# A fixed order for the seven products of a projection pair, a third buffer for weight splits, and three transfers moved

## The chip, the cores and the metric

The kernel runs on one core of a Trainium2 chip. The metric is the time of one execution on the device in microseconds (us). Engines are called as the profile calls them: PE (TensorE, matmuls; PEld is its weight load), DVE (VectorE), ACT (ScalarE), POOL (GpSimd) and SP (SyncE, which here only issues transfers). L353 is line 353 of the kernel before.

## What is computed

One inference step of a two-layer hybrid encoder. 512 prompt rows and 8 x 16 sample rows share the weights and are handled as T = 640 rows of width 1024. Cut to what matters here:

```python
for l in range(DEPTH):                      # DEPTH = 2
    (a_u, a_v, a_g, b_x, b_g, c_q, c_kv, c_kr, c_g, m_q, gate_logits) = split_cols(x @ w_in)
    oa = gelu(a_u) * mix(layer_norm(gelu(a_v))) * silu(a_g)      # gated mixing in chunks of 128
    ob = rglru(b_x) * silu(b_g)                                  # convolution of 4 + a recurrence
    oc = mla(c_q, c_kv, c_kr) * silu(c_g)                        # latent attention, past keys cached
    om = mem_attend(m_q, mem_k, mem_v)                           # memory attention, caches for samples
    g = sigmoid(gate_logits)                                     # four gates of 1024 columns
    merged = g[0]*(oa@w_br_a) + g[1]*(ob@w_br_b) + g[2]*(oc@w_br_c) + g[3]*(om@w_br_m)
    x = layer_norm(ALPHA * x + merged @ w_out)
```

## The kernel before

Every product is made three times in a reduced 32-bit format: a number is split into a high and a low part, and high x high, high x low and low x high are added. The split of a weight is done by `split` (L144): ACT casts the raw weight into `wh`, and DVE subtracts to get `wl` (L147). The buffers of `raw` are three, those of `wh`, `wl` and `ws` two each. Weights come on SP's queue, nearly all else (scratch in HBM written and read back) on POOL's queue, which works in its own order together with POOL's computations.

Most projections are taken two at a time by `fm_pair` (L353). It computes two chunks of 128 output rows for all 640 columns with seven products in place of eight, from sums of weights (DVE, L360) and sums of x (`xt`, computed once for each layer and kept in HBM as `xsum`). Each product is 12 matmuls of 128 x 320. In the order of the code they are, with the names used from here on:

- P1: x half 11 with `r0`, into `ba`, the first half of the accumulator tile `fp`; ACT then copies `ba` to `p1` (`tu`, L383).
- P2: x half 21 with `r0`, into `bb`, the second half of the same tile `fp`; DVE then adds z0 = p1 + bb (L377).
- P3: `xt[2]` with `ws`, added into `ba`; ACT copies it to `u` (`tu`, L392).
- P4: `xt[3]` with `ws`, into the separate bank `fp_c`; ACT copies it to z1 (L394).
- P5: `xt[1]` with `r1`, added into `ba`; DVE subtracts it from z1 (L377).
- P6: `xt[4]` with `r1`, added into `fp_c`; DVE forms the other half of z1 (L377).
- P7: x half 22 with the second half of `r0`, added into `ba`.

The accumulators `acc` (L80) are two tiles, shared by the pairs, the branch products `y`, the mixing `mix` and the single chunks `fm`. There are 40 pairs, 20 in a layer. Six stand in the front of the layer, in this order: two of u (`gelu_pair`, L419), two of gate C (`silu_pair(1, ...)`, L407), then the mixing, then two of gate B (`silu_pair(2, ...)`). Fourteen stand in the merge (`merge_pairs`, L1043): each computes two gate chunks and is followed by the branch products `y` of the same two chunks (48 matmuls of 128 x 320; 24 for the memory branch) and their multiply-adds on DVE. In PE's instruction order the products of a pair are woven into one another by a scheduler; the order section below shows it.

Between front and merge lie the latent attention, then the memory attention for the samples (four loads `mcache` of 1 MB from SP's queue, L809, in the three buffers of the pool `kv`), the recurrence (`lru_in`, `lru_gates`, `lru_rest` for four chunks), the memory attention for the prompt, and single chunks and products of the first merge branch. In the front, the u branch is written to scratch by `gelu_pair`, read back in four pieces `ub` (L566), multiplied with the mixed values and written back; pieces, copies `tu`, `mixb` and `th` share a pool of five buffers of 128 x 640 (`tmp`, L71). Gate B is read back as one tile `ob` of 4 x 640 (L804) for the whole recurrence, in the pool `o` in which the four reloaded `xt` (`x_sums_back`, L343, 1.25 MB each) also stand.

Of the kernel before, what the change touches and what calls it, by code (L numbers as in the profile page):

```python
# [22 lines left out]
NB = 8  # L23
# [16 lines left out]
def encoder_step(  # L40
# [65 lines left out]
    def whl(raw, n=1024):  # L106
        h, lo = wtile("wh", n, "wh"), wtile("wl", n, "wl")
        split(h, lo, raw)
        return h, lo
# [53 lines left out]
    def after(ins_, dep):  # L163
        tc.add_manual_dep(
            ins_.ins, dep.ins.name,
            mybir.DependencyInfo(mybir.DependencyClass.Sync, mybir.DependencyReason.DATA),
            reason="concurrent tiles of the array are issued together",
        )

# [9 lines left out]
    def spill(bi, k, src):  # L179
        nc.gpsimd.dma_start(out=oscr[bi][k], in_=src)  # L180
# [9 lines left out]
    for l in range(L):  # L190
# [66 lines left out]
        def w_c(c):  # L257
            if l > 0:
                r = wload(ins["w_c"][l, c], 832)
                x_sums(1)  # L260
                return r
            if c > 0:
                r = wload(ins["w_c"][l, c], 832)
                x_in(2 * c, 2)
                return r
            raw = wp.tile([128, 832], F32, tag="raw", name="raw", bufs=3)
            h = wp.tile([128, 832], F32R, tag="wh", name="wh")
            lo = wp.tile([128, 832], F32R, tag="wl", name="wl")
            for j in range(2):
                js = slice(416 * j, 416 * j + 416)  # L270
                nc.sync.dma_start(out=raw[:, js], in_=ins["w_c"][l, c][:, js])
                x_in(j, 1)
                split(h[:, js], lo[:, js], raw[:, js])
            return h, lo
# [68 lines left out]
        def x_sums_back():  # L343
            for i in range(4):
                t_ = otile([128, 2, 4, TH], F32R, f"xt{i}")
                nc.gpsimd.dma_start(out=t_.bitcast(F32), in_=xsum[i])
                xt[i + 1] = t_[:, 0], t_[:, 1]
# [5 lines left out]
        def fm_pair(c, take):  # L353

            r0, r1 = (wraw(ins["w_fm"][l, c + e]) for e in range(2))
            ws = wtile("ws", 1024, "ws")
# [8 lines left out]
            def product(o, hl, half, x, first, last):  # L365
# [3 lines left out]
                for n, (k, a, b) in enumerate(steps):  # L369
                    k0 = half * 512 + k * 128  # L370
                    PE.matmul(  # L371
                        out=o, lhsT=a[:, k0:k0 + 128], rhs=b[:, k, :],
                        start=(first and n == 0), stop=(n == len(steps) - 1), skip_group_check=True,
                    )

# [43 lines left out]
        def gelu_pair(c):  # L419
            gs = []  # L420
            z = fm_pair(FM_U + c, lambda e, cols, v_: gs.append((e, cols, v_)))
            for e, cols, v_ in gs:
                ACT.activation(out=z[e][:, cols], in_=v_, func=AF.Gelu_apprx_tanh)
            for e in range(2):
                nc.gpsimd.dma_start(out=gscr[0][c + e], in_=z[e])
# [75 lines left out]

        for c in (0, 2):
            gelu_pair(c)


        am = atile([128, 2560], F32, "am")
# [51 lines left out]
        for c in range(4):  # L558
# [6 lines left out]
            th, ub = tmp([128, T], "mixb"), tmp([128, T], "ub")  # L565
            nc.gpsimd.dma_start(out=ub, in_=gscr[0][c])  # L566
# [10 lines left out]
            DVE.tensor_tensor(out=ub, in0=ub, in1=th, op=ALU.mult)  # L577
            nc.gpsimd.dma_start(out=gscr[0][c], in_=ub)
# [218 lines left out]
        ob = gate_back(2, "ob")  # L797
# [9 lines left out]
        for bp in range(4):  # L807
            kv = kvtile([128, 2, 2, 2, 256], F32, "mcache")
# [75 lines left out]
        def lru_in(c):  # L884
            xp = lb[c % 2][:, 0, :]
# [45 lines left out]
        def lru_rest(c):  # L931
# [15 lines left out]
            DVE.tensor_tensor(out=ob[:, c, 0:NP_], in0=ob[:, c, 0:NP_], in1=xc[:, 0:NP_], op=ALU.mult)  # L947
            obs = ob[:, c, NP_:T].rearrange("p (b t) -> p b t", b=NB)
            DVE.tensor_tensor(out=obs, in0=obs, in1=samp(lb[c % 2][:, 1, :])[:, :, 0:TS], op=ALU.mult)
            spill(1, c, ob[:, c, :])  # L950
# [171 lines left out]
        lnp = [wtile("ws", 1024, f"lnp{i}") for i in range(2)]  # L1122
# [172 lines left out]
```

## Time and profile before

| what | value |
|---|---|
| three runs | 1450.77, 1454.91, 1456.23 us |
| median | 1454.91 us |
| the profiled execution itself | 1456.32 us, of which span 1454.6 us |
| busy share of the span | PE 96 %, DVE 68 %, ACT 45 %, POOL 9 % |
| mean granted TensorE clock | 0.990 of full speed |
| DMA | 189.2 MB, mean 130 GB/s |

The profiled execution lies 1.4 us above the median, so a sum made against it is moved by that much. A busy PE in this table is not PE at its peak: matmuls overlap, the recorded duration of one is 310 ns while the next starts 147 ns later, so short waits do not show as idle time. They are read from the distances of starts in the timeline.

### The profile page before, as it was taken

To read this page: it belongs to the slowest core of one execution; us is meant where nothing else is said; L and a number is where in the kernel's file an instruction comes from. 1 tells how busy PE (TensorE), PEld (TensorE's weight loads), DVE (VectorE), ACT (ScalarE), POOL (GpSimd) and SP (SyncE) were. 2 spreads that over 40 slices of the span, in tenths; PEclk is the share of its full clock that TensorE was granted. 3 is DMA by queue.
4 is the path that set the end of the run, shared out by engine and by line. 5 is a ranking of instruction groups with operands and counts; after the bars stand their busy time and mean duration, and the time that the engine had idled before them with its cause. 6 is when DMAs were issued, how large, how long until landed. Compare 5 with 4: busy or idle time off the path is not lost.

```text
span 1454.6 us, 22627 instructions
## 1 busy us (share of the span) xinstructions
PE 1396.1 (96%) x8896; PEld 1264.5 (87%) x8896; DVE 983.4 (68%) x1676; ACT 649.3 (45%) x1159; POOL 132.7 (9%) x270
## 2 busy tenths in 40 slices
PE   8997999999989999999999989999999999999997
PEld 8897988779979999998898979887799899999986
DVE  8676757766556676677785867577665566767766
ACT  6453544445534343445244535344555343434530
POOL 1102110012110000000112022000121100000000
PEclk9999999999999999999999989999999999999999
DMA  7645622433242233236365456224332533222332
GB/s 269 259 136 181 206 85 70 135 134 116 79 150 91 92 105 97 69 93 209 109 208 214 131 177 211 79 68 147 122 120 75 170 92 96 82 91 73 121 133 109
DMA packets 60379, 189.20 MB, mean 130 GB/s; under 512 B 6897, under 2 KB 16017, under 8 KB 57201
## 3 DMA queue, kind: packets, MB, share of 16 engines
q1 hardware_dynamic: 48304, 127.54, 27.9%
q0 software_dynamic: 11968, 60.22, 11.4%
q8 instruction: 70, 1.15, 0.3%
q14 instruction: 37, 0.30, 0.1%
HBM read 151.11 MB, written 35.31 MB: 128 GB/s over the span
## 4 chain that ended last, share of the span: by engine, by line
PE 78%; DVE 6%; DMA 5%; issue 5%; ACT 4%; POOL 1%; DVEq 0%; ACTq 0%; POOLq 0%; SPq 0%
PE fp L371 19%; PE fm L121 13%; PE y L121 12%; PE y_ps L1140 7%; PE fp_c L371 7%; PE v L136 4%; PE sc_ps L747 3%; ACT wh L146 2%; PE c L136 2%; PE pv_ps L771 2%; PE mem L136 2%; PE pt_ps L764 1%; PE q_ps L121 1%; DMA mcache<-in_mem_kv 1%; DMA ub<-gscr 1%
## 5 line engine op out<-in xcount | busy, mean ns | idle before, releaser
L146 ACT CAST wh<-raw 128x1024 fp32r<-128x1024 f32 (+3 forms) x215 | 198.7, 924 | 290.5 <-PE fp L371 88.0
L147 DVE TENSOR_TENSOR wl<-raw,wh 128x1024 fp32r<-128x1024 f32 (+3 forms) x215 | 228.7, 1064 | 71.1 <-ACT tu L392 26.4
L371 PE MATMUL fp<-xh,wh 128*128 128x320 f32 x480 | 148.1, 320 | 12.2 <-ACT tu L383 9.1
L121 PE MATMUL y<-bhl,wh 128*128 128x320 f32 x896 | 142.1, 309 | 1.5 <-ACT wh L146 1.1
L371 PE MATMUL fp<-xl,wh 128*128 128x320 f32 x480 | 143.4, 311 | 0.0
L121 PEld LDWEIGHTS y<-bhl,wh 128*128 128x128 f32 x896 | 133.9, 188 | 2.3 <-ACT wh L146 1.7
L371 PE MATMUL fp<-xt,wh 128*128 128x320 f32 x640 | 116.3, 325 | 11.3 <-DVE z L377 6.9
L371 PE MATMUL fp_c<-xt,wh 128*128 128x320 f32 x640 | 115.3, 313 | 6.4 <-DMA xt<-xsum 5.3
L371 PEld LDWEIGHTS fp<-xt,wh 128*128 128x128 f32 x640 | 96.4, 192 | 26.7 <-ACT tu L392 13.3
L121 PE MATMUL fm<-xh,wh 128*128 128x320 f32 x448 | 114.9, 327 | 0.0
L121 PE MATMUL fm<-xl,wh 128*128 128x320 f32 x448 | 113.3, 327 | 0.0
L371 PEld LDWEIGHTS fp<-xh,wh 128*128 128x128 f32 x480 | 90.6, 189 | 21.7 <-ACT tu L383 17.0
L371 PEld LDWEIGHTS fp_c<-xt,wh 128*128 128x128 f32 x640 | 100.0, 190 | 7.7 <-DMA xt<-xsum 5.8
L146 ACT CAST wh<-ws 128x1024 fp32r<-128x1024 f32 x40 | 42.0, 1051 | 120.9 <-PE y L121 84.9
L371 PEld LDWEIGHTS fp<-xl,wh 128*128 128x128 f32 x480 | 90.8, 189 | 0.1
L371 PE MATMUL fp<-xh,wl 128*128 128x320 f32 x480 | 90.4, 310 | 0.0
L121 PE MATMUL fm<-xh,wl 128*128 128x320 f32 x448 | 83.6, 323 | 0.0
L121 PEld LDWEIGHTS fm<-xh,wh 128*128 128x128 f32 x448 | 76.6, 191 | 7.4 <-issue 5.9
L121 PEld LDWEIGHTS fm<-xl,wh 128*128 128x128 f32 x448 | 76.2, 190 | 6.3 <-issue 4.5
L121 PE MATMUL y<-bhl,wl 128*128 128x320 f32 x448 | 76.6, 309 | 0.0
L371 PEld LDWEIGHTS fp<-xh,wl 128*128 128x128 f32 x480 | 75.8, 189 | 0.0
L121 PEld LDWEIGHTS fm<-xh,wl 128*128 128x128 f32 x448 | 68.1, 189 | 5.1 <-issue 4.4
(341 smaller groups left out, 2651.8 us busy)
## 6 DMA issues: line engine op xcount, KB each, us to landing
raw<-in_w_fm SPq DMA_DIRECT2D x108, 512.0 KB, 3.8
xsum<-xt POOLq DMA_DIRECT2D x8, 1280.0 KB, 10.6
xt<-xsum POOLq DMA_DIRECT2D x8, 1280.0 KB, 5.9
raw<-in_w_br SPq DMA_DIRECT2D x20, 512.0 KB, 3.6
mcache<-in_mem_kv SPq DMA_DIRECT2D x8, 1024.0 KB, 6.9
raw<-in_w_out SPq DMA_DIRECT2D x16, 512.0 KB, 4.3
osrc<-oscr POOLq DMA_DIRECT2D x20, 320.0 KB, 3.2
gscr<-th POOLq DMA_DIRECT2D x16, 320.0 KB, 2.9
```

The lines of the kernel that those rows point to most:

```text
L121: PE.matmul(out=out[:, j, 0:TH], lhsT=a(k), rhs=b(k)[:, j * TH:(j + 1) * TH], start=(n == 0), stop=(n == len(steps) - 1),)
L136: PE.matmul(out=o[:, 0:width], lhsT=a(ci * nk_per + j)[:, t * 128:(t + 1) * 128], rhs=w[:, j * width:(j + 1) * width], start=(ci == 0 and ...
L146: ACT.copy(out=dst_h, in_=src)
L147: DVE.tensor_tensor(out=dst_l, in0=src, in1=dst_h.bitcast(F32), op=ALU.subtract)
L371: PE.matmul(out=o, lhsT=a[:, k0:k0 + 128], rhs=b[:, k, :], start=(first and n == 0), stop=(n == len(steps) - 1), skip_group_check=True,)
L747: PE.matmul(out=s[:, 0:nk], lhsT=qT[0:kr_, h, ts_], rhs=kT[h // 4][0:kr_, h % 4, 0:nk], start=True, stop=True,)
L764: PE.transpose(tps[:, k * 128:(k + 1) * 128], p[:, k * 128:(k + 1) * 128], ident)
L771: mm = PE.matmul(out=ops[64 * e:64 * e + 64, hp * 128:(hp + 1) * 128], lhsT=vc[:, k, h * 64:(h + 1) * 64], rhs=pt[:, k * 128:(k + 1) * 128 ...
L1140: PE.matmul(out=o[j], lhsT=mg[k // 2][:, a, k % 2, t * 128:(t + 1) * 128], rhs=wo[k, w][:, j * 512:(j + 1) * 512], start=(k == 0 and p == ...
```

## The change

Six edits, all in the order of work and in where data stands; the arithmetic is the same.

1. `wh` has three buffers; `ws` has one, and the two layer-norm tiles `lnp`, which stood in `ws` buffers, stand in `wh` buffers.
2. `order_only` chains all matmuls of all pairs in the order of the code, for the scheduler alone: no wait is added.
3. The u branch is written by the Gelu into a tile `ub` on chip, which is the second half of an enlarged `am`, and multiplied in place there; one transfer writes it to scratch at the end. The two writes of a pair to scratch and the four reads are gone.
4. `x_sums_back` loads in the order 1, 2, 0, 3.
5. `mcache` takes buffers of the pool `o`.
6. Gate B of the recurrence is read back for each chunk in `lru_in`, into a `tmp` buffer, and the tile `ob` in the pool `o` is gone.

```diff
     def whl(raw, n=1024):
-        h, lo = wtile("wh", n, "wh"), wtile("wl", n, "wl")
+        h, lo = wtile("wh", n, "wh", 3), wtile("wl", n, "wl")
...
+    def order_only(ins_, dep):
+        if dep is not None:
+            tc.add_manual_dep(
+                ins_.ins, dep.ins.name,
+                mybir.DependencyInfo(mybir.DependencyClass.NoSync, mybir.DependencyReason.SCHED_ONLY),
+                reason="products of a pair stand in this order on the engine",
+            )
...
         def x_sums_back():
-            for i in range(4):
+            for i in (1, 2, 0, 3):
...
-            ws = wtile("ws", 1024, "ws")
+            ws = wtile("ws", 1024, "ws", 1)
...
-                    PE.matmul(
+                    mm = PE.matmul(
...
+                    order_only(mm, tail.get("p"))
+                    tail["p"] = mm
...
-                ACT.activation(out=z[e][:, cols], in_=v_, func=AF.Gelu_apprx_tanh)
-            for e in range(2):
-                nc.gpsimd.dma_start(out=gscr[0][c + e], in_=z[e])
+                ACT.activation(out=ub[:, c + e, cols], in_=v_, func=AF.Gelu_apprx_tanh)
...
+        am = atile([128, 5120], F32, "am")
+        ub = am[:, 2560:5120].rearrange("p (k t) -> p k t", k=4)
...
-            th, ub = tmp([128, T], "mixb"), tmp([128, T], "ub")
-            nc.gpsimd.dma_start(out=ub, in_=gscr[0][c])
+            th = tmp([128, T], "mixb")
...
-            DVE.tensor_tensor(out=ub, in0=ub, in1=th, op=ALU.mult)
-            nc.gpsimd.dma_start(out=gscr[0][c], in_=ub)
+            DVE.tensor_tensor(out=ub[:, c, :], in0=ub[:, c, :], in1=th, op=ALU.mult)
+        nc.gpsimd.dma_start(out=gscr[0].rearrange("k p t -> p k t"), in_=ub)
...
-        ob = gate_back(2, "ob")
+        ob = {}
...
-            kv = kvtile([128, 2, 2, 2, 256], F32, "mcache")
+            kv = otile([128, 2, 2, 2, 256], F32, "mcache")
...
         def lru_in(c):
+            ob[c] = tmp([128, T], "ob")
+            nc.gpsimd.dma_start(out=ob[c], in_=gscr[2][c])
...
-        lnp = [wtile("ws", 1024, f"lnp{i}") for i in range(2)]
+        lnp = [wp.tile([128, 1024], F32, tag="wh", name=f"lnp{i}", bufs=3) for i in range(2)]
```

PE, an ordinary merge pair of the first layer, from the end of P2 to the end of P6. `fp` with `xh`/`xl` is P2, with `xt1` P3, with `xt0` P5; `fp_c` with `xt2` is P4, with `xt3` P6 (a tile `xt1` is the sum that the code calls `xt[2]`, and so on). Before:

```order
L371 MATMUL fp_4752<-xh0_1_104,wl_4758 128x320 x4
L371 MATMUL fp_c_4753<-xt2_3997,wh_4790 128x320 x4
L371 MATMUL fp_c_4753<-xt2_3997,wl_4791 128x320
L371 MATMUL fp_4752<-xt1_3995,wh_4790 128x320 x8
L371 MATMUL fp_4752<-xt1_3995,wl_4791 128x320 x4
L371 MATMUL fp_c_4753<-xt2_3997,wl_4791 128x320 x3
L371 MATMUL fp_4752<-xt0_3993,wh_4820 128x320 x8
L371 MATMUL fp_4752<-xt0_3993,wl_4821 128x320 x4
L371 MATMUL fp_c_4753<-xt3_3999,wh_4820 128x320 x8
L371 MATMUL fp_c_4753<-xt3_3999,wl_4821 128x320 x4
```

After:

```order
L381 MATMUL fp_4926<-xh0_1_104,wl_4932 128x320 x4
L381 MATMUL fp_4926<-xt1_3984,wh_4964 128x320 x8
L381 MATMUL fp_4926<-xt1_3984,wl_4965 128x320 x4
L381 MATMUL fp_c_4927<-xt2_3986,wh_4964 128x320 x8
L381 MATMUL fp_c_4927<-xt2_3986,wl_4965 128x320 x4
L381 MATMUL fp_4926<-xt0_3988,wh_4994 128x320 x8
L381 MATMUL fp_4926<-xt0_3988,wl_4995 128x320 x4
L381 MATMUL fp_c_4927<-xt3_3990,wh_4994 128x320 x8
L381 MATMUL fp_c_4927<-xt3_3990,wl_4995 128x320 x4
```

Five matmuls of P4 stood between P2 and P3 and three between P3 and P5 (and four more of it ahead of P2, behind P1); now P1, P2 and P3 follow each other directly, and P4 stands whole between P3 and P5.

PE, the mixing products `mix` in the front of the first layer (the second layer is alike). `krT_ps` is a transpose, `fp_c` P4 of a pair of gate B; after, the first row is P7 of the second pair of gate C and the last is P1 of the next pair. Before:

```order
L561 MATMUL mix_1195<-am_872,v_290 128x128 x4
L371 MATMUL fp_c_1253<-xt3_302,wh_1290 128x320 x7
L561 MATMUL mix_1208<-am_872,v_290 128x128 x5
L561 MATMUL mix_1221<-am_872,v_290 128x128 x5
L371 MATMUL fp_c_1253<-xt3_302,wh_1290 128x320
L371 MATMUL fp_c_1253<-xt3_302,wl_1291 128x320 x4
L538 MATMUL krT_ps_1560<-ident_81,krp_514 128x128
L561 MATMUL mix_1234<-am_872,v_290 128x128 x5
```

After:

```order
L381 MATMUL fp_1066<-xh0_1_104,wl_1166 128x320 x4
L572 MATMUL mix_1191<-am_622,v_290 128x128 x2
L572 MATMUL mix_1201<-am_622,v_290 128x128 x5
L572 MATMUL mix_1211<-am_622,v_290 128x128 x5
L572 MATMUL mix_1221<-am_622,v_290 128x128 x5
L381 MATMUL fp_1237<-xh0_0_103,wh_1242 128x320
```

The last products of `mix` stood among matmuls of a pair; now seventeen of them stand in a row between P7 of one pair and P1 of the next.

POOL, the reload of the fourth `xt` in the first layer. `oscr1` is the write of a finished recurrence chunk to scratch (from `ob`), `oscr3` that of the memory branch, `osrc` a branch read back for the merge. Before:

```order
L945 COPY lh_3011<-lb1_3013 128x1
L946 COPY lh_3011<-lb1_3013 128x8
L1100 DMA out_lh<-lh_3011 128x144
L180 DMA oscr1_91<-ob_2854 128x640
L346 DMA xt3_3999<-xsum_94 128x2560
L1049 DMA osrc_4488<-oscr2_92 128x640
```

After:

```order
L190 DMA oscr1_91<-ob_2999 128x640
L907 COPY lh_2994<-lb0_2995 128x24
L896 DMA ob_3313<-gscr2_97 128x640
L896 DMA ob_3576<-gscr2_97 128x640
L190 DMA oscr3_93<-um_2726 128x640 x2
L356 DMA xt3_3990<-xsum_94 128x2560
L949 TENSOR_TENSOR a2_3555<-lb1_2996 128x664
```

The reload stood behind the last write of `ob`, at the end of the recurrence; now it stands behind the writes of the memory branch, ahead of POOL's work on the second chunk.

## Rows read from the trace of the kernel before

**Rows 1.** PE timeline, an ordinary merge pair, first layer: start us, us, instruction, count.

```profile
445.90 0.41 PE L371 MATMUL fp<-xh,wh 128*128 128x320 f32 x1
...
456.48 2.51 PE L121 MATMUL y<-bhl,wh 128*128 128x320 f32 x16
458.82 1.34 PE L121 MATMUL y<-bhl,wl 128*128 128x320 f32 x8
...
465.95 0.41 PE L371 MATMUL fp<-xh,wh 128*128 128x320 f32 x1
```

**Rows 2.** Stretches: window, length, busy and count for PE, PEld, DVE, ACT, POOL; clock.

```profile
392.00:423.40 31.40, 23.52 (x140) 21.81 (x139) 17.31 (x46) 13.93 (x19) 5.50 (x10) 0.95 0.39 129
423.40:672.00 248.60, 246.31 (x1623) 237.67 (x1622) 167.86 (x220) 105.64 (x160) 4.30 (x8) 1.00 0.33 100
1118.00:1145.00 27.00, 22.70 (x145) 21.03 (x144) 14.17 (x20) 14.05 (x18) 6.03 (x11) 1.00 0.43 147
1145.00:1393.00 248.00, 246.37 (x1622) 237.74 (x1621) 168.41 (x221) 105.47 (x160) 3.76 (x7) 1.00 0.34 102
```

**Rows 3.** PE timeline where P2 or P3 follows directly; in brackets idle before and releaser.

```profile
152.76 0.60 PE L371 MATMUL fp<-xh,wl 128*128 128x320 f32 x3
153.88 0.41 PE L371 MATMUL fp<-xh,wh 128*128 128x320 f32 x1 [0.52 <-ACT tu L383]
154.13 0.31 PE L371 MATMUL fp<-xl,wh 128*128 128x320 f32 x1
...
800.84 0.27 PE L538 MATMUL cqT_ps<-ident,cb 128*128 128x128 f32 x1
801.68 1.44 PE L371 MATMUL fp<-xt,wh 128*128 128x320 f32 x8 [0.57 <-DVE z L377]
```

**Rows 4.** Timelines of PE and ACT, first pair of gate B in either layer.

```profile
137.19 0.41 PE L371 MATMUL fp<-xh,wh 128*128 128x320 f32 x1 [2.56 <-ACT tu L383]
...
142.57 2.49 PE L371 MATMUL fp<-xt,wh 128*128 128x320 f32 x8 [3.37 <-DVE z L377]
144.86 1.27 PE L371 MATMUL fp<-xt,wl 128*128 128x320 f32 x4
...
863.88 0.64 PE L371 MATMUL fp<-xh,wh 128*128 128x320 f32 x1 [4.94 <-ACT tu L383]
...
868.10 2.50 PE L371 MATMUL fp<-xt,wh 128*128 128x320 f32 x8 [0.65 <-DVE z L377]
...
871.47 1.27 PE L371 MATMUL fp_c<-xt,wh 128*128 128x320 f32 x4
...
863.40 0.43 ACT L383 COPY tu<-fp 128x320 f32<-128x320 f32 x1 [12.56 <-DVE ub L577]
```

**Rows 5.** Timelines of DVE and PE around `mix`, first layer.

```profile
127.22 0.68 DVE L567 TENSOR_TENSOR mixb<-mix,am 128x512 f32<-128x512 f32 x1
127.82 0.28 DVE L572 TENSOR_TENSOR mixb<-mix,am 128x128 f32<-128x128 f32 x1
128.01 1.21 DVE L147 TENSOR_TENSOR wl<-ws,wh 128x1024 fp32r<-128x1024 f32 x1
129.15 0.81 DVE L577 TENSOR_TENSOR ub<-ub,mixb 128x640 f32<-128x640 f32 x1
...
131.51 1.35 PE L561 MATMUL mix<-am,v 128*128 128x128 f32 x10 [0.82 <-DVE mixb L572]
```

**Rows 6.** Timelines of PE and POOL, first merge pair, first layer.

```profile
399.93 1.44 PE L371 MATMUL fp<-xt,wh 128*128 128x320 f32 x8 [1.17 <-DVE z L377]
...
418.95 2.40 PE L371 MATMUL fp_c<-xt,wh 128*128 128x320 f32 x8 [4.40 <-DMA xt<-xsum]
...
410.93 0.54 POOL L346 DMA_DIRECT2D xt<-xsum  x1 [4.52 <-DMA oscr<-ob]
```

**Rows 7.** Waits of PE, whole span: in total us, times, longest; then the transfers' landing.

```profile
PE mss_ps L814 <- DMA mcache<-in_mem_kv: 5.9, 4, 2.6
...
DMA to landing us min/median/max: 4.8/6.9/8.8
```

More of the change, by code (lines that the diff above doesn't have):

```diff
@@ L168, in after @@
         )
+    def order_only(ins_, dep):
[5 more added lines that the diff above has]
+            )
+    tail = {}
     def halves(ap):
@@ L266, in w_c @@
             raw = wp.tile([128, 832], F32, tag="raw", name="raw", bufs=3)
-            h = wp.tile([128, 832], F32R, tag="wh", name="wh")
+            h = wp.tile([128, 832], F32R, tag="wh", name="wh", bufs=3)
             lo = wp.tile([128, 832], F32R, tag="wl", name="wl")
@@ L500, in encoder_step @@
             mem_kv()
+        am = atile([128, 5120], F32, "am")
+        ub = am[:, 2560:5120].rearrange("p (k t) -> p k t", k=4)
         for c in (0, 2):
             gelu_pair(c)
-        am = atile([128, 2560], F32, "am")
         nc.sync.dma_start(out=am[:, 0:1024], in_=ins["w_mix"][l])
@@ L946, in lru_rest @@
             POOL.tensor_copy(out=lh[:, c, 1:9], in_=xc[:, XP + TS - 1:XP + TS + (NB - 1) * XB:XB])
-            DVE.tensor_tensor(out=ob[:, c, 0:NP_], in0=ob[:, c, 0:NP_], in1=xc[:, 0:NP_], op=ALU.mult)
-            obs = ob[:, c, NP_:T].rearrange("p (b t) -> p b t", b=NB)
+            DVE.tensor_tensor(out=ob[c][:, 0:NP_], in0=ob[c][:, 0:NP_], in1=xc[:, 0:NP_], op=ALU.mult)
+            obs = ob[c][:, NP_:T].rearrange("p (b t) -> p b t", b=NB)
             DVE.tensor_tensor(out=obs, in0=obs, in1=samp(lb[c % 2][:, 1, :])[:, :, 0:TS], op=ALU.mult)
-            spill(1, c, ob[:, c, :])
+            spill(1, c, ob[c])
         def mem_prompt(i, last):
```

## The prediction

> **What bounds the kernel now.** I read the table of busy shares first: PE is busy for 96 % of the span, so the end is set by PE's own work plus the moments when PE waits. The change adds and takes no matmul; it only changes the waits. Since the recorded durations of matmuls overlap, I measure waits as distances of starts. Back to back, a 128 x 320 matmul starts every 147 ns: sixteen of `y` take from 456.48 to 458.82 [rows 1]. An ordinary merge pair has 84 matmuls of products and 48 of `y`, so 132 x 0.1467 = 19.36 us without any wait. From P2 to the next P2 it takes 445.90 to 465.95, 20.05 us [rows 1], so a pair loses about 0.7 us. The two long merge stretches say the same of all: 1623 and 1622 matmuls are 238.1 and 237.9 us of work in 248.6 and 248.0 us [rows 2], 20.6 us of waits for 26 pairs, **0.79 us for a pair**. The granted clock there is 1.00. The other waits are few and single: in the front at the first pair of gate B [rows 4], at the mixing [rows 5], in the first merge pair (its stretch is the first and the third line of the windows) [rows 2, 6], and for the memory caches [rows 7].
>
> **The fixed order.** `ba` and `bb` are halves of one tile, and any write to it waits for the last read of it, even of the other half. Where P2 follows P1 directly, PE waits for the copy of `ba` by ACT, though P2 writes only `bb`: the last matmul of P1 starts at 152.76 + 2 x 0.147 = 153.05 and P2 at 153.88, 0.83 us later where 0.147 would be the pace, and its second matmul comes at 0.25 instead of 0.147 [rows 3]. That is 0.68 + 0.10 = 0.78 us. Where P3 follows P2, it waits for DVE's z0: the last of P2 starts one step ahead of the transpose at 800.84, at 800.69, and P3 at 801.68; that is 0.99 - 0.147 = 0.84 us (the one transpose lies in it), with a slow second matmul (0.10, as above) 0.94; in the merge, where only part of P4 covered it, I read the same to within 0.05, and take 0.92. Before, the scheduler laid four matmuls of P4 behind P1, five behind P2 and three behind P3, and so paid 0.79 us in all. After, the order rows show P1, P2 and P3 bare, P4 whole between P3 and P5, P5 ahead of P6 and P6 ahead of P7. A whole product is 12 x 0.147 = 1.76 us, more than either wait, so the waits of P5, P6 and P7 go, and those of P2 and P3 are paid in full: **0.78 + 0.92 = 1.70 us for a pair, +0.91 against before**. For the 26 ordinary merge pairs that is +23.7 us. DVE and ACT have slack there (168 and 106 of 248.6 us busy, [rows 2]), so I expect z0 and the copies at the same distance as in rows 3.
>
> The Trainium skill, "PSUM — Partial Sum Buffer", section "PSUM bank collisions raise a hardware error", asks for semaphores by bank and quadrant, not by address; by that rule halves in different banks need no wait for each other. The rows show that here they do wait; by the rule alone the term would be below zero.
>
> **Front.** Twelve pairs. Ten are ordinary, at +0.91; three waits of P2 for ACT there were bare already (one is the 0.78 of rows 3, which was priced at about 0.2 in the average), so 10 x 0.91 - 3 x 0.6 = +7.3 us. The other two, the first pair of gate B in each layer, wait for the u branch: ACT's copy needs a `tmp` buffer that is held until DVE has multiplied a piece `ub` that comes back from scratch; ACT stood 12.56 us for that [rows 4]. PE lost 2.72 at 137.19 and 3.53 at 142.57 (the idle time in the bracket and 0.16, as 0.52 stands for 0.68 in rows 3), and the next 12 matmuls ran at the lower clock level, 8 in 2.29 us where 1.17 would do [rows 4]; for 12 that is 1.6 us. With the small waits of that pair, 8.2 us in the first layer. In the second, 5.10 at 863.88 and 0.81 at 868.10, and 28 matmuls at 267 to 280 ns, 3.37 us for the 12 that begin at 868.10 [rows 4], 0.12 to 0.13 us too much each: 9.6 us. Both go with `ub` on chip, and 1.70 us for the pair is left: -6.5 and -7.9. Against that the **mixing** stands bare after P7. With two accumulators, its second product waits for the gate of P7 (ACT and DVE, then the additions of the first), its fourth for the additions of the second, behind a `wl` and a multiplication on DVE, the next P1 for those of the third: 0.68 + 0.28 + 1.21 + 0.81 us are DVE's steps [rows 5], and I count 1.6 + 2.05 + 1.15 = 4.8 us in each layer. What it cost before is 0.98 at 131.51 [rows 5] and 1.0 for a split in the first layer, 0.7 in the second: +2.8 and +4.1. Three products of the mixing and four transposes now lie in the bare places and give back 0.8 in each layer. Front in all: 7.3 - 14.4 + 6.9 - 1.6 = **-1.8 us**.
>
> **First merge pair.** The fourth `xt` was requested only when the last write of `ob` had landed, at 410.93; PE waited 4.40 us for it and then ran 12 matmuls at the lower level [rows 6]. The stretch holds 140 matmuls, 20.5 us, in 31.40 us: 10.9 us of waits; in the second layer 145 in 27.00 us: 5.7 us [rows 2]. After, the load stands ahead of the recurrence's second chunk on POOL and nothing of `ob` is in its way. What stays is the pair's 1.70, P3's wait of 1.17 us and more, because z0 stands behind the recurrence on DVE [rows 6], and some of that for P6 and P7: 4.4 us. So -6.5 and -1.3, **-7.8 us**.
>
> **Memory caches.** PE waited 5.9 us in four places for the third and fourth cache [rows 7], and by the starts around them about 8.3 us with the clock that followed. In buffers of `o` three loads start long before; the fourth still waits for the first to be used, and its landing takes 6.9 us [rows 7] against some 6.4 us of PE work: 1 us is left in each layer. **-6 us.**
>
> **Nothing or little.** The third `wh` lets ACT cast earlier; PE waited for casts 2.7 us in all, one of them in the mixing: 0. One `ws`: its next sums come a whole pair later: 0. `lnp` in `wh` leaves one free buffer for the first splits of the second layer: +0.5, bounds 0 and 2. Gate B by pieces: four transfers of 320 KB instead of one, on POOL's queue, the second held until the memory branch frees a `tmp`; behind it wait the recurrence's steps on POOL. No row shows that; I take 0, between -3 and +3.
>
> **Sum.** 23.7 - 1.8 - 7.8 - 6 + 0.5 = +8.6 us on the profiled 1456.3, so 1464.9; the median lies 1.4 lower: **1463.5 us**, +0.6 %. My bounds on the price of a pair (1.5 to 1.9) move it by 8 either way, the mixing by 2, the rest by 3: 1454 to 1474 for this case.
>
> **Rivals.** (a) *The order pays.* If the new order let P2 and P3 start without their waits (the halves followed apart), each of the 40 pairs would lose about 0.1 instead of the forecast's 1.70: 1463.5 - 40 x 1.6 + 1.6 (nothing is left to give back in the front) = 1401 us. For it speaks only that the halves hold different data; against it rows 3, where just this order was run and waited. (b) *The gains are larger than the waits.* If the caches leave nothing, the mixing costs 2 instead of 4.8 in each layer, and z0 comes sooner behind a freer DVE (1.5 for a pair): 8.6 - 2 - 5.6 - 8 = -7, 1448 us, faster. (c) *ACT becomes late.* With P1 bare, P2 hangs on one ACT instruction. If a cast of `ws` or `r1` (1 us) still stands in ACT ahead of the copy `p1`, because its `wh` buffer comes free only with the `y` products, P2 waits up to 0.4 us more in each of 40 pairs, +16: 1479. It decides when the cast begins less than a microsecond before P1 ends; the third buffer speaks against it. (d) *The clock falls.* If two waits of 0.8 us in each pair took PE to the lower level for 12 matmuls, 1.5 us a pair, 26 pairs cost 39 us: 1502. Rows 3 speak against it: after 0.83 us the second matmul followed at 0.25 and the stretch of the merge has 1.00; only after 3.4 us and more did the pace fall [rows 4, 6]. The Trainium skill, "TensorE: Matmul & The Clock Gate", section "A second HAM failure mode: psum-queue depth-cycling", tells of such short idles between groups that make the clock swing; no wait of this size does it in these rows.
>
> **How the numbers follow.** Forecast 0.53, (a) 0.07, (b) 0.17, (c) 0.18, (d) 0.05. A difference under 0.5 % (7.3 us, below 1447.6 or above 1462.2) can hardly be told from none. The forecast lies on that upper edge: of its 0.53 I give 0.29 to slower and 0.24 to same; of (b) 0.11 to faster and 0.06 to same; (a) is faster, (c) and (d) slower. Faster 0.18, same 0.30, slower 0.52. The range takes the forecast, most of (b) and two thirds of (c): 1446 to 1482.
>
> **What would show it.** In the profile after: gaps of about 0.7 to 0.8 us ahead of every P2 (released by the copy `tu`) and every P3 (by z0), none ahead of P5, P6 and P7, and a merge pair of 21.0 instead of 20.05 us; no wait of ACT for `ub`, no 1.2 GHz stretch in the front; three waits around `mix` of 1 to 2 us; no wait for `xt`; at most one short one for `mcache` in each layer. Wrong it would be made by a merge pair of 20 us or less (then (a) or (b)), or by waits for `tmp`, `wh` or POOL that stand nowhere before.

## The result

| kernel | median of four runs | range |
|---|---|---|
| before | 1454.59 us | 1450.77 to 1456.23 |
| changed | 1472.08 us | 1471.14 to 1476.25 |

The ratio is **1.013, 95 % interval 1.010 to 1.016**: slower by 17.5 us, where the prediction said +8.6. The direction was right and the time lies in the range; the size was twice the forecast. The profiled execution of the changed kernel took 1476.25 us (span 1474.5), 19.9 us more than that of before, and the working below is against these two. It is the slowest of the four, 4.2 us above their median, so single waits in its trace can be longer than is usual.

From the page of the changed kernel, the busy shares and the two costliest groups of the pairs' products (busy and mean ns of one; idle time ahead and what ended most of it):

```profile
PE 1383.2 (94%) x8896; PEld 1256.6 (85%) x8896; DVE 984.0 (67%) x1676; ACT 650.2 (44%) x1159; POOL 124.5 (8%) x254
...
L381 PE MATMUL fp<-xh,wh 128*128 128x320 f32 x480 | 147.3, 319 | 27.1 <-ACT tu L395 23.5
...
L381 PE MATMUL fp<-xt,wh 128*128 128x320 f32 x640 | 110.9, 315 | 26.3 <-DVE z L389 26.3
```

PE is busy 94 % instead of 96 %, with the same matmuls. One ordinary merge pair in the PE timeline of the changed kernel (start, duration, instruction, count; idle before and releaser in brackets), the counterpart of [rows 1]:

```profile
438.09 0.75 PE L381 MATMUL fp<-xh,wl 128*128 128x320 f32 x4
439.35 0.41 PE L381 MATMUL fp<-xh,wh 128*128 128x320 f32 x1 [0.52 <-ACT tu L395]
...
440.63 0.75 PE L381 MATMUL fp<-xh,wl 128*128 128x320 f32 x4
442.01 1.44 PE L381 MATMUL fp<-xt,wh 128*128 128x320 f32 x8 [0.64 <-DVE z L389]
...
460.39 0.41 PE L381 MATMUL fp<-xh,wh 128*128 128x320 f32 x1 [0.52 <-ACT tu L395]
```

P1's last four matmuls begin at 438.09, so P2 is due at 438.68 and starts at 439.35. P2's last four begin at 440.63, so P3 is due at 441.22 and starts at 442.01. Nothing waits between P3 and the next P1. From P2 to P2 it is 439.35 to 460.39, **21.04 us, against 20.05 before; the prediction said 21.0.** So the main term was right, and the missing 11 us (19.9 against 8.6) lie elsewhere. The largest waits of PE over the whole span (total us, times, longest):

```profile
PE fp L381 <- DVE z L389: 28.8, 41, 1.5
PE fp L381 <- ACT tu L395: 23.5, 36, 1.3
...
PE y L121 <- ACT lb L905: 3.3, 2, 1.7
PE mso_ps L844 <- ACT pt_ms L839: 2.9, 1, 2.9
...
PE mem L136 <- ACT v L507: 2.4, 1, 2.4
```

The first two are the bare P3 and P2. The waits for `xt` and `mcache` [rows 6, 7] have no row any more. Of the waits that no line of the prediction names, the three largest are for ACT: `y` for the recurrence's copy `lb` and `mso_ps` for `pt_ms` are new, and that of the memory projection `mem` for the gelu of `v` was 0.8 us before. Smaller ones are for DVE: `k_ps` in the latent attention 2.3 us instead of 1.0, and 1.6 us for each of `gate` and `y_ps`, which had none.

To find where the time went I cut the span in each layer at the first start of `fp`, the last `fp` of the front, and the first starts of `mss_ps`, of `fp` in the merge pairs, and of `y_ps`; layer 2 begins with its first `mem`. "Casts held" and "best" are kernels of the experiments below.

| stretch, us | before | changed | difference | casts held | best |
|---|---|---|---|---|---|
| layer 1: start to first pair | 70.4 | 73.4 | +3.0 | 69.8 | 70.2 |
| layer 1: front | 94.3 | 93.4 | -0.9 | 94.3 | 85.1 |
| layer 1: memory attention and recurrence | 106.9 | 104.0 | -2.9 | 101.8 | 102.6 |
| layer 1: merge pairs | 278.7 | 285.3 | +6.6 | 282.9 | 258.2 |
| layer 2: start | 65.6 | 65.3 | -0.3 | 65.4 | 64.9 |
| layer 2: front | 94.2 | 92.7 | -1.6 | 91.8 | 83.3 |
| layer 2: memory attention and recurrence | 106.9 | 109.0 | +2.1 | 101.8 | 103.6 |
| layer 2: merge pairs | 272.3 | 283.9 | +11.6 | 282.4 | 257.8 |
| the rest (latent attention, output) | 365.3 | 367.5 | +2.2 | 367.4 | 363.6 |

### The profile page after: what moved, and what is told of

It reads as the page before. It is cut to its first block, busy times and chain, and to the rows that moved or that the text cites. A ratio compares the mean times of both kernels' runs of the same rounds, so it can differ in the third digit from the quotient of the medians.

```text
span 1474.5 us, 22634 instructions
## 1 busy us (share of the span) xinstructions
PE 1383.2 (94%) x8896; PEld 1256.6 (85%) x8896; DVE 984.0 (67%) x1676; ACT 650.2 (44%) x1159; POOL 124.5 (8%) x254
## 5 line engine op out<-in xcount | busy, mean ns | idle before, releaser
L381 PE MATMUL fp<-xt,wh 128*128 128x320 f32 x640 | 110.9, 315 | 26.3 <-DVE z L389 26.3
L121 PE MATMUL fm<-xh,wh 128*128 128x320 f32 x448 | 111.7, 323 | 0.0
L381 PE MATMUL fp_c<-xt,wh 128*128 128x320 f32 x640 | 106.9, 309 | 0.0
L121 PE MATMUL fm<-xh,wl 128*128 128x320 f32 x448 | 87.2, 327 | 0.0
```

The costliest lines, as they stand in the source:

```text
L121: PE.matmul(out=out[:, j, 0:TH], lhsT=a(k), rhs=b(k)[:, j * TH:(j + 1) * TH], start=(n == 0), stop=(n == len(steps) - 1),)
L381: mm = PE.matmul(out=o, lhsT=a[:, k0:k0 + 128], rhs=b[:, k, :], start=(first and n == 0), stop=(n == len(steps) - 1), skip_group_check=True,)
```

## The experiments

Every kernel was timed against the kernel before on the same chip, whose median there was 1452.8 to 1455.8 us. The runs stand on several chips, so differences between two kernels are good to some 3 us: taken from the ratios in place of the times they move by up to that. Diffs are against the changed kernel, if not said otherwise.

### The order of the products

**The order alone**, put into the kernel before:

```diff
-                    PE.matmul(
+                    mm = PE.matmul(
...
+                    order_only(mm, tail.get("p"))
+                    tail["p"] = mm
```

> The kernel before with the fixed order added and nothing else. Theory A: 0.91 us for each of some 38 pairs, the bare mixing 2 us a layer, while the waits of the first gate B pair for the u branch and of the first merge pair for xt stay: 1454.6 + 35 to 42, so 1490 to 1497 us. Rival B (with two buffers of wh and woven loads the order costs less than the steps say): 1470 to 1480 us, which would put the loss on the other edits.

Measured 1504.22 us (ratio 1.033, 1.032 to 1.035), +50 and 7 us above the upper end. The excess is one wait in each layer, in PE's list of this kernel (23.0 us against 5.3 before) and on POOL in its first merge pair:

```profile
PE fp_c L381 <- DMA xt<-xsum: 23.0, 2, 11.7
...
412.70 0.54 POOL L190 DMA_DIRECT2D oscr<-ob  x1
418.25 0.54 POOL L356 DMA_DIRECT2D xt<-xsum  x1 [5.01 <-DMA oscr<-ob]
```

Before, this wait was 4.40 us in the first layer [rows 6] and 0.9 in the second. P6, which wants the fourth `xt`, now stands ahead of P7 and of the pair's `y`, and these can't fill it any more: a fixed order turns a late operand into a full stop.

**The change without the order:**

```diff
-                    order_only(mm, tail.get("p"))
-                    tail["p"] = mm
```

> The changed kernel without the fixed order alone; the other five edits stay. Theory A (bare waits of P2 and P3, as in the trace after: 0.78 and 0.92 us a pair): with P4 woven in again 26 merge pairs get back 0.9 us each, five memory-branch pairs 0.7 more, the front some 6: 33 us, 1436 to 1446 us, a merge pair of about 20.1 us instead of 21.05. Rival B (the new transfers and buffers cost the time, not the order): 1465 us or more, with a merge pair that is shorter but new waits elsewhere.

Measured 1429.19 us (0.982, 0.979 to 0.984): without the order the rest of the change gains 25 us, and the order costs 43, more than theory A's 33.

**A bank of its own for P2**, the order kept:

```diff
-            ba, bb = (ab[:, j, 0:TH] for j in range(2))
+            ba, bb = ab[:, 0, 0:TH], bank_s("fp_b")[:, 0:TH]
```

> The changed kernel with one line altered: P2 writes the second bank of the pool s instead of the second half of the accumulator tile. Theory A (P2 and P3 wait only because the halves share one tile): both waits go although the order stays, a merge pair takes 19.4 to 19.6 us instead of 21.05, and the time is 1402 to 1415 us. Rival B (the waits belong to the order itself: PE needs the copy or z0 for other reasons, or the bank is then missed elsewhere): a merge pair stays at 21 us or the waits move to fp_b and fp_c; 1455 to 1475 us.

Measured 1397.80 us (0.961, 0.959 to 0.963), 4 us below theory A's range. The same pair in its PE timeline:

```profile
440.81 0.75 PE L381 MATMUL fp<-xh,wl 128*128 128x320 f32 x4
441.40 0.31 PE L381 MATMUL fp_b<-xh,wh 128*128 128x320 f32 x1
...
442.57 0.75 PE L381 MATMUL fp_b<-xh,wl 128*128 128x320 f32 x4
443.16 1.33 PE L381 MATMUL fp<-xt,wh 128*128 128x320 f32 x8
...
460.17 0.75 PE L381 MATMUL fp<-xh,wl 128*128 128x320 f32 x4
```

P2 follows P1 and P3 follows P2 at the pace (0.59 us for four matmuls), and the pair takes 440.81 to 460.17, 19.36 us: 132 matmuls and no wait. So both waits came only from P1 and P2 being halves of one tile. **The same line in the kernel before:**

> The kernel before with P2 in its own bank and nothing else: no fixed order, two wh buffers, all transfers as before. Theory A: the scheduler needs no weaving, 26 merge pairs lose their 0.79 us and the front pairs theirs (about 28 us in all), while the waits for the u branch, the caches and the reloaded xt stay: 1424 to 1434 us. If the products of y can no longer pass the late xt, up to 18 us of that come back: 1445 us. Rival B (the bank helps only with the other edits): 1450 to 1456 us.

Measured 1418.46 us (0.976, 0.974 to 0.978), 6 us below theory A's range. With that bank in place the whole change gains 20.7 us (1418.46 to 1397.80), where without it it loses 17.5.

### The third buffer

**Two buffers of `wh` and two of `ws` again:**

```diff
-        h, lo = wtile("wh", n, "wh", 3), wtile("wl", n, "wl")
+        h, lo = wtile("wh", n, "wh", 2), wtile("wl", n, "wl")
...
-            ws = wtile("ws", 1024, "ws", 1)
+            ws = wtile("ws", 1024, "ws", 2)
...
-        lnp = [wp.tile([128, 1024], F32, tag="wh", name=f"lnp{i}", bufs=3) for i in range(2)]
+        lnp = [wtile("ws", 1024, f"lnp{i}") for i in range(2)]
```

> The changed kernel with two buffers for high weight parts, two for weight sums and the layer-norm tiles among the sums, as before; the order stays fixed. Theory A (the third buffer puts a cast earlier in ACT's queue, where it holds up the work behind it): the wait of 2.4 us ahead of the memory projection at 60.5 us and the lower clock behind it go (3 us), the two waits of y for the recurrence (1.6 us each) shrink, P2's wait of 1.26 us in memory-branch pairs falls to 0.68: 5 to 10 us less, 1462 to 1467 us. Rival B (the third buffer is neutral or helps the pairs): 1472 us or more.

Measured 1456.45 us (1.0005, 0.9995 to 1.0015). The pools cost 15.6 us, more than the theory's upper end. **Two of `wh`, but one `ws`** (and `lnp` in a tile of `o`) tells which pool:

> The changed kernel with two buffers of wh, but one buffer for the weight sums as in the change, and the layer-norm tiles in a tile of the pool o. It parts what the run with two buffers undid together. Theory A (the third wh buffer is what costs): 1453 to 1460 us. Rival B (the single buffer of sums, which holds the next sums and with them ACT's cast back, is what costs): 1466 to 1475 us.

Measured 1458.16 us (1.002, 1.001 to 1.003): it is the third `wh`, 13.9 us. How an additional buffer can cost time is read at the start of the changed kernel. First ACT, then PE, then the stretch from 60.5 to 65 us (length; busy of PE, PEld, DVE, ACT, POOL with counts; granted clock; DMA):

```profile
57.03 1.05 ACT L146 CAST wh<-raw 128x1024 fp32r<-128x1024 f32 x1 [2.71 <-PE v L136]
58.09 1.28 ACT L507 ACT_TABLE_LOAD   x1
59.39 2.56 ACT L507 ACTIVATE v<-v 128x512 f32<-128x512 f32 x5
...
60.52 0.91 PE L136 MATMUL mem<-wh,mem_h 128*128 128x512 f32 x2 [2.44 <-ACT v L507]
...
60.50:65.00 4.50, 4.47 (x13) 3.56 (x14) 3.08 (x9) 2.40 (x4) 0.00 (x0) 0.62 0.25 102
```

The cast at 57.03 is that of the third memory weight, which PE wants only at 67.75. With two buffers the scheduler lets two memory weights go ahead of the gelus, with three buffers three. The third waits there; the table load and the gelus of `v` stand behind it and can't pass. PE, which wants their banks, stops for 2.44 us, and then runs at a granted clock of 0.62.

The bracket names PE, but what came late was the transfer of this weight. It was issued at 51.79 and landed 5.1 us later, at 56.93, 0.1 us ahead of the cast. In the kernel with a bank for P2, which has three buffers and the same order of ACT here, it landed after 3.2 us, the cast began at 55.47, PE waited 0.8 us for `mem`, and the first pair began at 70.3 us. First the transfer in the changed kernel, then the cast in the one with the bank:

```profile
DMA to landing us min/median/max: 5.1/5.1/5.1
...
55.47 1.05 ACT L146 CAST wh<-raw 128x1024 fp32r<-128x1024 f32 x1 [1.15 <-PE v L136]
```

So the third buffer lays the gelus open to a late transfer; the 3.0 us at this start are in part those of this execution. The same in the recurrence of the first layer, where the kernel with the bank has the same wait of 4.82 us: ACT, then PE.

```profile
350.38 0.95 ACT L947 ACTIVATE lb<-lb,sn 128x664 f32<-128x664 f32 x1
356.14 1.05 ACT L146 CAST wh<-raw 128x1024 fp32r<-128x1024 f32 x1 [4.82 <-DMA raw<-in_w_fm]
357.22 1.28 ACT L951 ACT_TABLE_LOAD   x1
358.51 0.76 ACT L951 ACTIVATE lb<-lb 128x664 f32<-128x664 f32 x1
...
362.61 0.29 ACT L905 COPY lb<-fm 128x128 f32<-128x128 f32 x1
...
362.95 2.32 PE L121 MATMUL y<-bhl,wh 128*128 128x320 f32 x14 [1.64 <-ACT lb L905]
```

A cast for the next weights stands ahead of the square root (L951) and waits 4.82 us for its transfer; the root, the scan behind it on DVE and the copy `lb` come late, and `y` waits. And in a merge pair of the memory branch:

```profile
624.45 1.03 ACT L146 CAST wh<-raw 128x1024 fp32r<-128x1024 f32 x1
625.38 0.41 ACT L395 COPY tu<-fp 128x320 f32<-128x320 f32 x1
...
625.85 0.42 PE L381 MATMUL fp<-xh,wh 128*128 128x320 f32 x1 [1.10 <-ACT tu L395]
```

Here a cast begins just ahead of the copy of P1, and P2's idle time is 1.10 instead of 0.52.

**Three buffers, the casts held where two would put them** separates the place in the queue from the buffer. The scheduler is told to place each cast after the last product that reads the high part two before it; at run time nothing is added:

```diff
-        split(h, lo, raw)
+        cast = ACT.copy(out=h, in_=raw)
+        if tail.get("hold"):
+            order_only(cast, last_use.get(high[-2]) if len(high) > 1 else None)
+        high.append(h.tensor.name)
+        DVE.tensor_tensor(out=lo, in0=raw, in1=h.bitcast(F32), op=ALU.subtract)
```

(`last_use` is filled by a wrapper of the matmul call with the last reader of each tile; the profile gives most matmuls of this and the next two kernels the wrapper's line, L55.)

> The changed kernel with its three buffers, and one thing else: in ScalarE's own queue each cast of a high part is kept behind the last product that reads the high part two before it, which is where two buffers put it. This orders the instructions as they are scheduled; no semaphore is added and no buffer taken away. Theory A, the third buffer costs its 14 to 16 us through the place in ScalarE's queue that the cast takes (it waits there for its transfer or for its buffer, with gelus, square roots and copies behind it): the time falls to that of the run with two buffers, 1456.5, so 1455 to 1460 us. Rival B, the third buffer costs by itself (where the tiles lie, what the norm weights of the layer's end do in its slots, when the weight transfers start): the queue's order does not matter and the time stays at 1470 to 1474 us. In between, both: the share is read off.

Measured 1458.72 us (1.003, 1.002 to 1.004): 13.4 of the 15.6 us come back with all three buffers in place. **The cost comes through the order of ACT's queue, not through the buffer itself.** The same two places, ACT and PE at the start, ACT and PE in the recurrence:

```profile
52.81 1.06 ACT L121 CAST wh<-raw 128x1024 fp32r<-128x1024 f32 x1 [1.18 <-DMA raw<-in_w_mem]
53.88 1.28 ACT L525 ACT_TABLE_LOAD   x1
57.28 2.56 ACT L525 ACTIVATE v<-v 128x512 f32<-128x512 f32 x5 [2.11 <-PE v L55]
...
58.42 0.74 PE L55 MATMUL mem<-wh,mem_h 128*128 128x512 f32 x2
...
348.27 0.60 ACT L121 CAST wh<-raw 128x512 fp32r<-128x512 f32 x1
348.90 1.28 ACT L969 ACT_TABLE_LOAD   x1
350.66 0.76 ACT L969 ACTIVATE lb<-lb 128x664 f32<-128x664 f32 x1 [0.48 <-DVE lb L968]
...
358.20 2.51 PE L55 MATMUL y<-bhl,wh 128*128 128x320 f32 x16
```

The gelus wait for PE's product and for nothing else, the root comes 0.48 us after its table and waits there for DVE, and `mem` and `y` start with no wait. **Held in the first part of each layer only**: the text below says up to the first merge pair, but `tail["hold"]` is set false ahead of the recurrence, so the casts of the recurrence, of the prompt's memory attention and of the first merge branch are free as well:

> As the run before it, but the casts are held only up to the first merge pair of each layer; in the merge pairs they stand where the third buffer lets them. Theory A: what the third buffer costs in the merge pairs (2.9 us in layer 1 and 1.5 in layer 2, by the stretches of the changed kernel and of the run with two buffers) stays, the rest, 8 to 11 us, goes: 1459 to 1464 us. Rival B, most of the cost comes from the merge pairs: 1467 to 1472. Rival C, the early casts in the merges cost nothing once the rest is in place: 1455 to 1458.

Measured 1463.31 us (1.006, 1.004 to 1.009): 8.8 us of the cost go with the casts held ahead of the recurrence, 4.6 stay with those behind it. Against the run with all casts held, the two stretches of memory attention and recurrence are longer by 3.5 us together and the merge pairs by 1.9. So the time lies in theory A's range, but the 4.4 us that it put into the merge pairs are not all there.

### The other edits, each put back into the kernel with two buffers

**The u branch through scratch** (the two transfers out of `gelu_pair` and the pieces back):

```diff
-                ACT.activation(out=ub[:, c + e, cols], in_=v_, func=AF.Gelu_apprx_tanh)
+                ACT.activation(out=z[e][:, cols], in_=v_, func=AF.Gelu_apprx_tanh)
+            for e in range(2):
+                nc.gpsimd.dma_start(out=gscr[0][c + e], in_=z[e])
...
+            nc.gpsimd.dma_start(out=ub, in_=gscr[0][c])
```

> As the run with two wh buffers (1456.5 us, order fixed), but the u branch goes through scratch again, in four pieces, as before. Theory A (ACT's copy waits for a tmp buffer that a piece holds): waits of 2.5 to 5 us at the first pair of gate B and the lower clock behind them come back, 6 to 8 us in each layer: 1468 to 1474 us. Rival B (with the mixing bare behind P7 the pieces come in time): 1456 to 1460 us.

Measured 1466.69 us (1.008, 1.007 to 1.010), 1.3 us below theory A's range: keeping it on chip gains 10.2 us. **The memory caches in `kv`:**

```diff
-            kv = otile([128, 2, 2, 2, 256], F32, "mcache")
+            kv = kvtile([128, 2, 2, 2, 256], F32, "mcache")
```

> As the run with two wh buffers (1456.5 us), but the memory caches in the three buffers of the pool kv, as before. Theory A (the third and fourth cache come late): waits for mcache of 0.5 to 2.6 us and the lower clock behind them return, 3 to 4 us in each layer: 1462 to 1465 us. Rival B (the recurrence behind it sets the pace of this stretch, and the caches' waits are hidden in it): 1456 to 1459 us.

Measured 1466.20 us (1.009, 1.007 to 1.011): the caches' place gains 9.7 us, where the prediction said 6. **Gate B whole, `xt` read back 0 to 3:**

```diff
-            for i in (1, 2, 0, 3):
+            for i in range(4):
...
-        ob = {}
+        ob = gate_back(2, "ob")
+        ob = {c: ob[:, c, :] for c in range(4)}
...
-            ob[c] = tmp([128, T], "ob")
-            nc.gpsimd.dma_start(out=ob[c], in_=gscr[2][c])
```

> As the run with two wh buffers (1456.5 us), but gate B of the recurrence as one tile of the pool o again and the reloads in the order 0 to 3. Theory A (with a fixed order P6 waits for the late xt and y waits behind P6): one wait for xt of 9 to 12 us in each layer, as in the run with the order alone: 1475 to 1482 us. Rival B (the reload finds its buffer in time): 1456 to 1462 us.

Measured 1486.74 us (1.023, 1.021 to 1.025), +30.3 and 5 us above theory A's range. The waits of the three kernels, from the lists of the first two (with two buffers alone the first is 28.4, the longest 1.6) and the PE timeline of the third:

```profile
PE fp L381 <- DVE z L389: 34.1, 38, 4.4
...
PE mss_ps L824 <- DMA mcache<-in_mem_kv: 6.0, 4, 3.1
...
413.20 2.47 PE L381 MATMUL fp_c<-xt,wh 128*128 128x320 f32 x8 [11.38 <-DMA xt<-xsum]
```

Each edit put back brings its own wait back; the last also brings one of 1.3 us for `mcache`, and it holds two of the six edits, which no run took apart. **No order and two buffers** leaves edits 3 to 6 alone:

> Neither the fixed order nor the third buffer: what the transfers and tiles moved (u branch on chip, memory caches, gate B by pieces, order of the reloads) are worth alone. Theory A (the third buffer costs in any order, by casts ahead of the recurrence's steps on ACT): 1414 to 1424 us, under the 1429.2 without the order alone. Rival B (the third buffer helps a woven order): 1429 to 1440 us. By the steps of the prediction, the moved parts are worth 14 (u branch), 8 (xt) and 6 us (caches): 1427 us.

Measured 1421.63 us (0.977, 0.975 to 0.978), as theory A said: the useful part of the change is worth 33 us. The third buffer costs 7.6 us here (1429.19 less 1421.63), half of its 15.6 beside the order.

### A version that beats both

**Own bank and two buffers**, then **own bank and a third buffer for the pair's third weights only** (`w1 = whl(r1, tag="wh1")`, with `lnp` in `o`):

> P2 in its own bank and two buffers of wh together (two ws, layer-norm tiles among them), the rest of the change as it is. Theory A (the two losses are separate: bare waits in the pairs, and casts ahead of other work in ACT's queue): 1397.8 less the 15.6 us that two buffers gave back, 1380 to 1386 us. Rival B (the third buffer only cost where P2 hung on ACT's copy): 1393 to 1400 us.

> P2 in its own bank, and the third buffer for the pairs alone: two wh buffers for all, and a buffer of its own for the split of r1; the layer-norm tiles in a tile of the pool o. Theory A (a third buffer is worth 2 us in each merge, and costs where the recurrence and the memory attention wait for ACT): the merges as with three buffers (0.4 and 0.1 us of waits), the rest as with two: 1389 to 1393 us, under both runs with the bank (1397.8 and 1395.5). Rival B (the order of ACT changes again elsewhere): 1395 to 1400 us.

Measured 1395.49 us (0.959, 0.958 to 0.960) and 1395.60 us (0.960, 0.958 to 0.962). Both times the time fell in the rival's range, in the first run not for the rival's reason: two buffers save 3 to 5 us in each memory stretch and lose some 2 us in each merge, so that the third buffer costs only 2.3 us in all; the third buffer for the pairs takes that away, but the fronts grew by 3 us each, for which I have only the trace's new waits and no further run. **Own bank, three buffers, casts held up to the recurrence:**

> As the run before it, with the own bank for the second product besides. Theory A: the start and the memory stretches are as short as with two buffers and own bank (1395.5), and the merge pairs wait for nothing as with three (1397.8), which were 2.2 and 2.0 us shorter: 1390 to 1394 us. Rival B, the two cannot be had together, as when a third buffer was given to the pair's third weights alone (1395.6): 1395 to 1400 us.

Measured **1390.55 us (0.956, 0.955 to 0.958)**, in theory A's range; the interval touches those of the two runs above. Against own bank and two buffers the merges are shorter by 2.0 and 1.8 us, as it said, but the memory stretches are longer by 1.6 and 1.4, and 3.9 us were gained in the latent attention, which it did not name. The merges of its first layer (the stretch):

```profile
380.00:637.00 257.00, 256.53 (x1746) 255.73 (x1745) 183.14 (x263) 117.89 (x175) 9.09 (x17) 1.00 0.33 103
```

1746 matmuls at 147 ns are 256.2 us of the 257.0: next to nothing is left to take from the waits of the merge.

## Why the prediction was right and wrong

**The order: right.** 0.68 + 0.10 ahead of P2 and 0.79 + 0.11 ahead of P3, 1.68 us together, where 1.70 was forecast (the second term is the late second matmul: the first takes 0.41 instead of 0.31 us, the eight of P3 1.44 instead of 1.33); P5 to P7 wait for nothing. The waits of one rare place [rows 3] gave the price of 26 regular ones. For the merges the sum was 23.7 - 7.8 = +15.9 us; the table has +18.2, and +14.3 with casts held.

**The rule on PSUM** weighed in the prediction ("PSUM — Partial Sum Buffer", section "PSUM bank collisions raise a hardware error", of the Trainium skill) asks for semaphores by bank. Here the waits follow the tile: they stand in every pair while P1 and P2 share one, and are gone when P2 has its own.

**Front: right in sum, wrong in parts.** -2.5 us measured, -1.8 forecast. At the mixing PE stood idle 2.2 us in the first layer, some 2.7 by the distances of starts, little more than half of the 4.8 that I added up from DVE's steps:

```profile
132.38 2.50 PE L572 MATMUL mix<-am,v 128*128 128x128 f32 x20 [1.55 <-DVE th L425]
135.34 1.35 PE L572 MATMUL mix<-am,v 128*128 128x128 f32 x10 [0.46 <-DVE mixb L582]
136.87 0.38 PE L381 MATMUL fp<-xh,wh 128*128 128x320 f32 x1 [0.18 <-DVE mixb L582]
```

The u branch, -14.4 in my sum, gave 10.2 us in its own run.

**Memory caches: right in kind, too small.** Forecast -6; the trace of after has no wait for `mcache` at all, and putting them back costs 9.7. But the stretches fell by only 2.9 and rose by 2.1 us. A part of that is a price of this very edit which I did not see (below, at the split of `oa`); the rest leads to the step that failed.

**The step that failed** is "The third `wh` lets ACT cast earlier; PE waited for casts 2.7 us in all, one of them in the mixing: 0." It measured +15.6 us beside the fixed order (13.4 of it by the queue's order alone), 7.6 without the order and 2.3 with a bank for P2. I asked what an earlier cast could gain and never what is queued behind it. ACT takes its instructions in order; a cast that is free to go early is put ahead of a gelu, a square root or a copy, and when its transfer or its buffer is late, all of them are late. I had the mechanism in hand as rival (c), but only for the copy of P1 in a pair, and let "the third buffer speaks against it" stand, which was the wrong way round: the third buffer made it, in a few pairs (at 624.45) and above all outside of them, where I had not looked. With the casts held, the profiled span is 1457.7 us, +3.1 against before, less than the +8.6 of the sum, mostly by the caches (-10.2 instead of -6 in the two memory stretches, and with two buffers the caches put back make these stretches 11.5 us longer). The +2.2 us of the rest of the span, where I had 0.5, stay with the casts held. The trace has the waits for DVE there (`k_ps`, `y_ps`), but no run took them apart.

**The edits add up.** The order +49.6, gate B and `xt` -30.3, caches -9.7, u branch -10.2, third buffer +15.6 make +15.0; measured is +17.5. The 2.5 us between lie within the spread of the chips; each price holds beside the edits it was taken with. The price of `xt`, -7.8 in my sum, is not at odds with -30.3: most of that is a wait that the order itself makes (11.38 us where it was 4.40), and the order and the earlier load were costed together.

**Rivals.** (a) needs the halves to be followed apart; it happened only with the own bank, at 1397.8 us where (a) said 1401. (b) did not come. (c) came in another place, as said. (d) is refuted: the pairs' stretches keep a clock of 1.00.

**A price of the caches' place.** In the second layer's memory attention of the changed kernel ACT stood still 4.38 us ahead of a split of `oa` with no releaser shown, and PE then waited 2.95 us for `pt_ms`. First ACT, PE and the stretch behind, with its clock; then the landing of the four writes of `oc` to scratch, issued from 1014.68 to 1016.31; last the same split with two buffers:

```profile
1025.05 0.74 ACT L149 ACTIVATE bhl<-oa 128x640 fp32r<-128x640 f32 x1 [4.38 <-issue]
...
1026.10 0.64 PE L844 MATMUL mso_ps<-mcache,pt_ms 128*32 128x128 f32 x16 [2.95 <-ACT pt_ms L839]
...
1026.10:1031.00 4.90, 4.90 (x46) 3.94 (x47) 3.50 (x6) 3.61 (x7) 0.00 (x0) 0.65 0.02 7
...
DMA to landing us min/median/max: 2.5/3.8/8.6
...
1015.16 0.74 ACT L149 ACTIVATE bhl<-oa 128x640 fp32r<-128x640 f32 x1 [3.07 <-issue]
```

The last of the four writes landed 8.6 us after its issue, at 1024.90, and the split began 0.15 us later: both its target and `oc` are tiles of the pool `o`. With two buffers the same write landed at 1015.0 and the split began at 1015.16. In the four kernels with the caches in `kv` (before, the order alone, the bank alone, the caches put back) the four splits are done some 20 us ahead of the memory attention and wait for nothing. So this wait comes with `mcache` in the pool `o`, whatever the number of `wh` buffers, and the changed kernel met a late landing. With the casts held the split stands behind the next copy of `pt_ms`, the wait of PE is not in the list and the stretch is 101.8 us; so some of the 13.4 us are this split's place, and no run parts the two.

## What to carry to other kernels

A deeper pool is not free on an in-order engine: whatever it lets go earlier moves ahead of other work in that engine's queue, so for each freed instruction look at what it will wait for (transfer, slot) and at what stands behind it; keep the depth and pin the place. An order fixed by hand takes away the filling, so first remove the waits that the scheduler was filling: with two products in halves of one tile the order cost 43 us (35 with two buffers). The fastest version, with a bank for each, has the same order, but no run with that bank and the other edits leaves the order out, so whether it gains anything there is not shown. Ahead of a fixed order every operand must come in time, since nothing fills in any more.

## What the runs showed of the hardware

In the changed kernel the clock fell behind the two longest single waits alone. After PE's 2.44 us at 60.52 the granted clock of the next 4.5 us was 0.62, after the 2.95 us at 1026.10 it was 0.65 for 4.9 us (between the levels of 2.4 and 1.2 GHz, so most of each stretch at the lower); from 65 us on it was 1.00 again. The prediction had looked at waits of 3.4 us and more alone [rows 4, 6]; shorter ones did it here. Two waits of 1.32 and 1.47 us in the first merge pair, less than four microseconds apart, left it at 1.00 (PE, then the stretch). The length of a wait alone does not decide it: in the kernel without the order a wait of 2.24 us that ended at 752.35 left the next 5 us at 1.00, and one of 1.93 us that ended at 999.18 was followed by 4.8 us at 0.65.

```profile
396.00 0.42 PE L381 MATMUL fp<-xh,wh 128*128 128x320 f32 x1 [1.32 <-ACT tu L395]
...
399.50 1.43 PE L381 MATMUL fp<-xt,wh 128*128 128x320 f32 x8 [1.47 <-DVE z L389]
...
396.00:402.00 6.00, 4.53 (x29) 4.26 (x30) 3.51 (x5) 5.26 (x7) 1.59 (x3) 1.00 0.10 14
```

So a late cast of some two microseconds costs more than itself: the start is 3.6 us shorter with the casts held, and the wait was 2.44. The Trainium skill ("TensorE: Matmul & The Clock Gate", section "A second HAM failure mode: psum-queue depth-cycling") warns of short idles between groups of products; in these traces no pair, with its two idles of 0.5 to 0.6 us, shows a lower clock.
